# A queue-order planner without a reserve for the matrix engine, choosing among 60 orders

## The chip, the cores and the metric

The kernel runs on one core of one Trainium2 chip. The metric is the time of one execution on the device in microseconds (us); lower is better. The core's engines work side by side, each through its own queue in order: PE (TensorE, matrix products and transposes), DVE (VectorE), ACT (ScalarE), POOL (GpSimd), and SP (SyncE), which only issues transfers (DMA). PE reads its operands from SBUF and writes to eight PSUM banks, named `bk0` to `bk7` here.

## The reference, cut to what matters

One step of a four-layer trunk, D = 2048, on 128 context tokens and 256 latent tokens. Layers 0 and 3 mix with windowed attention, layer 1 with neighbourhood attention (16 heads of 128 each), layer 2 with a gated MLP.

```python
for i in range(DEPTH):                      # 4 layers, mixer i % 3
    kind = i % N_MIXERS
    sh, sc, gt = split(silu(cond) @ w_ada[i] + b_ada[i], 3)   # for c_ctx and for c
    h = rmsnorm(x, norm_g[i]) * (1 + sc) + sh
    if kind in (0, 1):                      # window / neighbourhood attention
        q, k, v, z = split(h @ w_in)
        y = (attention(rmsnorm(q), rmsnorm(k), v, cache) * silu(z)) @ w_out
    else:                                   # gMLP in chunks of 128 positions
        u, v, z = split(h @ w_in)           # gelu on u and v
        y = (u * mix(layernorm(v)) * silu(z)) @ w_out
    x = x + gt * y
```

All data are 32-bit floats.

## The kernel before, in words

**Tiling.** x is held transposed, feature by token: 16 blocks of 128 x 384. Every weight comes as 128 x 1024 tiles of 512 KB into one of four buffers `raw`. Each tile is split in two by `split`: ACT writes the rounded `H`, DVE writes the remainder `L` = `raw` - `H` (three buffers of each). The activations are split likewise into `hH` and `hL`. A product is then three matmuls, hH·H, hL·H and hH·L, added up in a PSUM bank. These matmuls of a layer's weights are called the main stream below.

**Attention heads.** Beside the main stream of layers 0, 1 and 3 run the 16 heads of that layer. A head (`head`) comes to PE in pieces that are here called chunks: transposes of q into a bank; the scores (`bk<-pair,qT`), which need `qT` and `qc` from DVE and ACT; seven transposes of the normalized weights `Pt` or `PH` (heads alternate between these two tiles); then the product with v (`bk<-pc,cv`, `bk<-PTH,pair`, `bk<-PLT,pair`), which needs `PTH` and `pc` from ACT and `PLT` from DVE. Between scores and transposes DVE and ACT do the softmax: row maxima into `sm`, exponentials, the RECIPROCAL of the sums, and the scaling of `Pt`. At a layer's end stands `W_out`: its results leave the bank by DVE's `pair<-bk,ada,pair` (gate times product, added to x).

**The modulation stream ("ada rows").** The modulation vectors of layers 1 to 3 are mostly made without PE: 272 tiles `araw` of w_ada, for each a DVE product `prod<-araw,cbc` for one condition and `araw<-araw,cbc` for the other, each summed by an ACT instruction with an accumulator; the sums go through `accA` to `ada`. These 544 DVE and 544 ACT instructions are not urgent: each layer's vectors are read only when the layer before it ends.

**What sets the order.** The kernel is first written out by generators in program order, and class `Rec` only records each operation. `Rec.cost` gives a modelled duration, `add` the dependencies. `due` works out, back from PE's times, by when each operation must have begun for PE not to wait. `schedule` then simulates the five engines and picks, on each engine, from the operations whose inputs are there: PE takes them in program order (chunks of heads may move against the main stream), the others the one that is due first. `ready_at` says when an operation's inputs are there: the end of the producer plus `SEM` = 45 ns when it is on another engine, and for PE's operations `MARGIN` = 250 ns more. `order` runs `due` and `schedule` three times, each from the times of the last, and `emit` issues the operations in the order of the planned starts. All recorded instructions therefore bear one line of the code: 322 before, 355 after. The planner runs when the kernel is built; on the chip the queues run by themselves, and an operation that comes to the head of its queue too early waits there, with all behind it.

Of the kernel before, what the change touches and what calls it, by code (L numbers as in the profile page):

```python
# [3 lines left out]

# [45 lines left out]
class Rec:  # L50
# [162 lines left out]
                have = set(x for x, _ in self.dep[c])  # L213
                self.dep[c] += [(x, d) for x, d in self.dep[i] if x < c and x not in have]

    def ready_at(self, i, start, done, margin=0):
        t, e = 0.0, self.eng[i]
        for x, data in self.dep[i]:
            v = start[x] + 1
            if data:  # L220
                v = done[x] + (35 if self.eng[x] == e else self.SEM if e else self.SEM + margin)
            if v > t:
                t = v
        return t
# [28 lines left out]
                    late[x] = v  # L253
        return late

    MARGIN = 250

    def schedule(self, late, land=4000):
        n = len(self.ops)
        succ, left = [[] for _ in range(n)], [0] * n  # L260
        for i in range(n):
            left[i] = len(self.dep[i])
            for x, _ in self.dep[i]:
                succ[x].append(i)
        start, done = [0.0] * n, [0.0] * n
        free, dma = [0.0] * 5, 0.0
        wait, ready = [[] for _ in range(5)], [[] for _ in range(5)]
        key = [(float(i) if self.chunk[i] == i else -1.0) if self.eng[i] == 0 else late[i] for i in range(n)]
        for i in range(n):
            if not left[i]:  # L270
                heapq.heappush(wait[self.eng[i]], (0.0, i))
        count = 0
        while count < n:
            best, be = None, None
            for e in range(5):
                if ready[e]:
                    t = free[e]
                elif wait[e]:
                    t = max(free[e], wait[e][0][0])
                else:  # L280
                    continue
                if best is None or t < best:
                    best, be = t, e
            e, t = be, best
            while wait[e] and wait[e][0][0] <= t:
                i = heapq.heappop(wait[e])[1]
                heapq.heappush(ready[e], (key[i], i))
            i = ready[e][0][1]
            if e in (1, 2) and wait[e]:
                end, hold = t + self.dur[i], None  # L290
                for est, j in wait[e]:
                    if est < end and late[j] < end and late[j] < late[i] and (hold is None or est < hold):
                        hold = est
                if hold is not None:
                    free[e] = hold
                    continue
            heapq.heappop(ready[e])
            start[i] = t
            free[e] = t + self.dur[i]
            if self.load[i]:  # L300
                dma = max(dma, t + 700) + self.load[i]
                done[i] = max(dma + land, t + self.lat[i])
            else:
                done[i] = t + self.lat[i]
            count += 1
            for s in succ[i]:
                left[s] -= 1
                if not left[s]:
                    heapq.heappush(wait[self.eng[s]], (self.ready_at(s, start, done, self.MARGIN), s))
        return start, done  # L310

    def order(self, passes=3):
        self.join()
        start, done = self.in_order()
        for _ in range(passes):
            start, done = self.schedule(self.due(start))
        return sorted(range(len(self.ops)), key=lambda i: (start[i], i))

    def emit(self):
        for i in self.order():  # L320
# [1443 lines left out]
```

## Time and profile before

| what | before |
|---|---|
| runs, median (lowest to highest) | 2989.2 us (2988.85 to 2990.47), 3 runs |
| profiled execution, its own time | 2990.54 us |
| its span in the trace | 2988.7 us |
| PE busy, share of the span | 2954.1 us, 99% |
| DVE busy | 2127.0 us, 71% |
| ACT busy | 1742.6 us, 58% |
| mean granted clock of PE | 0.997 |

A busy share is an average over the span: DVE is at nine tenths or more in most of the first half and at half of that afterwards. PE's waits are listed with what released them. The granted clock is given as a share of 2.4 GHz; 0.5 is the other level, 1.2 GHz, and a value between is a stretch that holds some of both. A row `L322 PE MATMUL bk<-hH,H ...` reads: line, engine, operation, tile written, tiles read.

### The profile page before, as it was taken

Reading aid. Unit: us, or ns where it says so; the run is one execution under the profiler, and the core shown is the slowest. Engines: PE = TensorE matmul, PEld = TensorE weight load, DVE = VectorE, ACT = ScalarE, POOL = GpSimd, SP = SyncE. Lnnn points to the kernel's source line nnn. Section 1 sums busy time; section 2 is a strip of 40 time slices with the busy share of each in tenths; the row PEclk is TensorE's granted clock in tenths of the full one; section 3 lists DMA queues with packets and bytes.
Section 4 is the critical chain, followed back from the end, with each engine's and each line's share of the span. In section 5 each row is a group of like instructions: output and inputs, shape, how many; then the busy total and the mean of one; then the engine's idle time right before and its main releaser. Section 6 shows DMA issues by size and latency. Waiting matters only on the chain.

```text
span 2988.7 us, 43977 instructions
## 1 busy us (share of the span) xinstructions
PE 2954.1 (99%) x16504; PEld 2703.4 (90%) x16504; DVE 2127.0 (71%) x3158; ACT 1742.6 (58%) x3340; POOL 79.9 (3%) x45
## 2 busy tenths in 40 slices
PE   7999999999999999999999999999999999999999
PEld 4789999978888888997888999999999988899999
DVE  4599999989989999998994833433455456455664
ACT  3388888778888888777883222222233235454542
POOL 0000000000101010000000000000000000000000
PEclk9999999999999999999999999999999999999999
DMA  9866677867776777887774544344454454333433
GB/s 379 343 227 220 201 236 251 279 242 257 235 252 234 257 239 255 286 263 287 260 260 134 176 128 124 124 126 128 124 169 141 144 191 134 123 106 106 138 111 126
DMA packets 187359, 598.96 MB, mean 200 GB/s; under 512 B 21764, under 2 KB 47620, under 8 KB 187140
## 3 DMA queue, kind: packets, MB, share of 16 engines
q1 hardware_dynamic: 186712, 596.00, 59.8%
q8 instruction: 129, 2.11, 0.3%
q14 instruction: 86, 0.70, 0.1%
q10 hardware_dynamic: 432, 0.13, 0.0%
HBM read 580.31 MB, written 15.75 MB: 199 GB/s over the span
## 4 chain that ended last, share of the span: by engine, by line
PE 95%; DVE 2%; ACT 1%; DMA 1%; issue 1%; DVEq 0%; SPq 0%; ACTq 0%
PE bk L322 95%; DVE prod L322 0%; DVE L L322 0%; DVE pair L322 0%; DVE Pt L322 0%; DMA pair<-i_xT 0%; ACT prod L322 0%; ACT Pt L322 0%; DMA aux<-i_relb 0%; DMA sel<-i_sel 0%; ACT H L322 0%; DVE PH L322 0%; DVE PLT L322 0%; ACT PH L322 0%; DVE araw L322 0%
## 5 line engine op out<-in xcount | busy, mean ns | idle before, releaser
L322 ACT ACTIVATE H<-raw 128x1024 fp32r<-128x1024 f32 x640 | 677.7, 1059 | 957.3 <-PE bk L322 887.7
L322 DVE TENSOR_TENSOR L<-raw,H 128x1024 fp32r<-128x1024 f32 x640 | 784.6, 1226 | 465.7 <-ACT H L322 460.7
L322 PE MATMUL bk<-hH,H 128*128 128x384 f32 x3072 | 1035.7, 337 | 5.5 <-DVE pair L322 5.4
L322 PE MATMUL bk<-hH,L 128*128 128x384 f32 x3072 | 1028.5, 335 | 0.0
L322 PE MATMUL bk<-hL,H 128*128 128x384 f32 x3072 | 1027.8, 335 | 0.0
L322 PE MATMUL bk<-H,hH 128*128 128x512 f32 x1536 | 605.6, 394 | 6.8 <-ACT hH L322 5.4
L322 PE MATMUL bk<-H,hL 128*128 128x512 f32 x1536 | 601.1, 391 | 0.3 <-DVE hL L322 0.3
L322 PE MATMUL bk<-L,hH 128*128 128x512 f32 x1536 | 600.6, 391 | 0.1
L322 PEld LDWEIGHTS bk<-hH,H 128*128 128x128 f32 x3072 | 577.1, 188 | 15.1 <-DVE pair L322 7.4
L322 PEld LDWEIGHTS bk<-hL,H 128*128 128x128 f32 x3072 | 577.2, 188 | 0.7
L322 PEld LDWEIGHTS bk<-hH,L 128*128 128x128 f32 x3072 | 576.9, 188 | 0.4 <-DVE cbc L322 0.4
L322 PEld LDWEIGHTS bk<-H,hH 128*128 128x128 f32 x1536 | 289.1, 188 | 71.5 <-ACT hH L322 6.6
L322 DVE TENSOR_TENSOR prod<-araw,cbc 128x1024 f32<-128x1024 f32 x272 | 335.6, 1234 | 16.6 <-ACT prod L322 11.4
L322 PEld LDWEIGHTS bk<-H,hL 128*128 128x128 f32 x1536 | 288.9, 188 | 64.2 <-issue 1.3
L322 PEld LDWEIGHTS bk<-L,hH 128*128 128x128 f32 x1536 | 289.2, 188 | 57.9 <-issue 1.3
L322 DVE TENSOR_TENSOR araw<-araw,cbc 128x1024 f32<-128x1024 f32 x272 | 335.4, 1234 | 5.0 <-DMA cbc<-srow 1.5
L322 ACT ACTIVATE prod<-prod 128x1024 f32<-128x1024 f32 x272 | 287.1, 1055 | 62.6 <-DVE prod L322 52.3
L322 ACT ACTIVATE araw<-araw 128x1024 f32<-128x1024 f32 x272 | 286.8, 1054 | 39.2 <-DVE araw L322 38.3
L322 DVE SCALAR_TENSOR_TENSOR pair<-bk,ada,pair 128x256 f32<-128x256 f32 x320 | 119.1, 412 | 178.1 <-PE bk L322 177.9
L322 ACT ACTIVATE pair<-bk 128x512 f32<-128x512 f32 (+2 forms) x150 | 82.0, 556 | 22.4 <-PE bk L322 21.9
L322 DVE TENSOR_TENSOR PLT<-bk,aux 128x384 f32<-128x384 f32 x32 | 17.8, 557 | 73.4 <-PE bk L322 73.3
L322 DVE TENSOR_TENSOR pair<-pair,aux 128x512 f32<-128x512 f32 (+1 forms) x108 | 59.1, 589 | 12.2 <-ACT pair L322 11.9
(152 smaller groups left out, 2048.6 us busy)
## 6 DMA issues: line engine op xcount, KB each, us to landing
araw<-i_w_adaT SPq DMA_DIRECT2D x272, 512.0 KB, 4.4
raw<-i_win_B SPq DMA_DIRECT2D x96, 512.0 KB, 3.7
raw<-i_nat_B SPq DMA_DIRECT2D x96, 512.0 KB, 4.3
pair<-i_w_ada SPq DMA_DIRECT2D x77, 512.0 KB, 7.2
raw<-i_win_O SPq DMA_DIRECT2D x64, 512.0 KB, 3.8
raw<-i_gm_V SPq DMA_DIRECT2D x64, 512.0 KB, 4.3
raw<-i_gm_U SPq DMA_DIRECT2D x64, 512.0 KB, 3.6
raw<-i_gm_Z SPq DMA_DIRECT2D x64, 512.0 KB, 3.6
```

The costliest lines, as they stand in the source:

```text
L322: getattr(getattr(self.real, e), op)(*a, **k)
```

## The change

`MARGIN` is gone: PE's operations count as ready 45 ns after their last producer, as those of the other engines do. `order` makes 60 orders instead of 3. Six come from the old iteration, each from the times of the last. For the other 54, the due times of the best order so far are shifted at random by up to 1.2 us either way, for the operations of DVE, ACT, POOL and SP that start in the 200 us before a random point, and a new order is planned from them. Every order gets a mark: the planned end, plus the ends of three trials (`trial`), which replay the order with durations up to 3% longer, results up to 120 ns later and loads landing after 3000 instead of 4000 ns. The order with the lowest mark is issued. The recorded operations and their dependencies are the same as before; only their places in the queues differ.

```diff
-    def ready_at(self, i, start, done, margin=0):
+    def ready_at(self, i, start, done):
...
-                v = done[x] + (35 if self.eng[x] == e else self.SEM if e else self.SEM + margin)
+                v = done[x] + (35 if self.eng[x] == e else self.SEM)
...
-    MARGIN = 250
+    def trial(self, order, seed):
+
+        rnd = random.Random(seed)
+        free, dma = [0.0] * 5, 0.0
+        start, done = [0.0] * len(order), [0.0] * len(order)
+        for i in order:
+            e = self.eng[i]
+            t = max(free[e], self.ready_at(i, start, done))
+            start[i] = t
+            more = self.dur[i] * 0.03 * rnd.random() if e else 0
+            free[e] = t + self.dur[i] + more
+            if self.load[i]:
+                dma = max(dma, t + 700) + self.load[i]
+                done[i] = max(dma + 3000, t + self.lat[i])
+            else:
+                done[i] = t + self.lat[i] + more + (120 * rnd.random() if e else 0)
+        return max(done)
...
-                    heapq.heappush(wait[self.eng[s]], (self.ready_at(s, start, done, self.MARGIN), s))
+                    heapq.heappush(wait[self.eng[s]], (self.ready_at(s, start, done), s))
...
-    def order(self, passes=3):
+    def order(self, passes=60):
         self.join()
+        rnd = random.Random(1)
         start, done = self.in_order()
-        for _ in range(passes):
-            start, done = self.schedule(self.due(start))
-        return sorted(range(len(self.ops)), key=lambda i: (start[i], i))
+        best = None
+        for n in range(passes):
+            if n < 6:
+                late = self.due(start)
+            else:
+                w = max(done) * rnd.random()
+                late = [x + (rnd.random() - 0.5) * 2400 if self.eng[i] and 0 < w - start[i] < 2e5 else x
+                        for i, x in enumerate(best[2])]
+            new, done = self.schedule(late)
+            o = sorted(range(len(self.ops)), key=lambda i: (new[i], i))
+            end = max(done) + sum(self.trial(o, k) for k in range(3))
+            if n < 6:
+                start = new
+            if best is None or end < best[0]:
+                best, start = (end, o, late), new
+        return best[1]
```

**Place 1, PE at the end of layer 0's heads.** From the scores of one head (tile `qT`) to the transposes of `Pt_228`, the normalized weights of the head before it, and on to that head's product with v. Before:

```order
L322 MATMUL bk4_118<-pair3_169_296,qT_79 128x384
L322 MATMUL bk5_119<-ident_84,Pt_228_355 128x128 x4
L322 MATMUL bk2_116<-ident_84,Pt_228_355 128x128 x3
L322 MATMUL bk6_120<-hH_65,H0_71 128x384
L322 MATMUL bk6_120<-hL_66,H0_71 128x384
L322 MATMUL bk6_120<-hH_65,L0_74 128x384
L322 MATMUL bk6_120<-hH_65,H0_71 128x384
L322 MATMUL bk6_120<-hL_66,H0_71 128x384
L322 MATMUL bk6_120<-hH_65,L0_74 128x384
L322 MATMUL bk5_119<-pc_81,cv_160_287 128x128
```

And now:

```order
L355 MATMUL bk4_118<-pair3_169_296,qT_79 128x384
L355 MATMUL bk1_115<-hL_66,H2_73 128x384
L355 MATMUL bk1_115<-hH_65,L2_76 128x384
L355 MATMUL bk1_115<-hH_65,H2_73 128x384
L355 MATMUL bk1_115<-hL_66,H2_73 128x384
L355 MATMUL bk1_115<-hH_65,L2_76 128x384
L355 MATMUL bk1_115<-hH_65,H2_73 128x384
L355 MATMUL bk5_119<-ident_84,Pt_228_355 128x128 x4
L355 MATMUL bk2_116<-ident_84,Pt_228_355 128x128 x3
L355 MATMUL bk1_115<-hL_66,H2_73 128x384
L355 MATMUL bk1_115<-hH_65,L2_76 128x384
```

Before, nothing stood between the scores and the transposes, and 6 matmuls of the main stream between the transposes and `bk5<-pc,cv`; now 6 stand ahead of the transposes and 18 behind them, and the transposes are PE's row 2062 where they were row 2082.

**Place 2, DVE in layer 1.** From the RECIPROCAL of a head's sums to that head's `PLT_377`, with `L0`, `L1` for the main stream and ada rows (`prod`, `araw`) in between. Before:

```order
L322 RECIPROCAL sm0_106<-sm0_106 128x3
L322 TENSOR_SCALAR Pt_375_502<-Pt_375_502,sm0_106 128x384
L322 TENSOR_TENSOR prod_77<-araw2_322_449,cbc_78 128x1024
L322 TENSOR_TENSOR araw2_322_449<-araw2_322_449,cbc_78 128x1024
L322 TENSOR_TENSOR L0_74<-raw3_70,H0_71 128x1024
L322 TENSOR_TENSOR prod_77<-araw0_323_450,cbc_78 128x1024
L322 TENSOR_TENSOR araw0_323_450<-araw0_323_450,cbc_78 128x1024
L322 TENSOR_TENSOR L1_75<-raw0_67,H1_72 128x1024
L322 TENSOR_TENSOR PLT_377_504<-bk5_119,PTH_376_503 128x512
L322 TENSOR_TENSOR PLT_377_504<-bk6_120,PTH_376_503 128x256
```

And now:

```order
L355 RECIPROCAL sm0_106<-sm0_106 128x3
L355 TENSOR_SCALAR Pt_375_502<-Pt_375_502,sm0_106 128x384
L355 TENSOR_TENSOR L0_74<-raw3_70,H0_71 128x1024
L355 TENSOR_TENSOR prod_77<-araw0_317_444,cbc_78 128x1024
L355 TENSOR_TENSOR L1_75<-raw0_67,H1_72 128x1024
L355 TENSOR_TENSOR PLT_377_504<-bk5_119,PTH_376_503 128x512
L355 TENSOR_TENSOR PLT_377_504<-bk6_120,PTH_376_503 128x256
```

Of four ada rows between the two, one is left; the others stand later in DVE's queue.

**Place 3, PE where layer 1's last heads meet W_out.** Around the transposes of `Pt_415` and the use of bank `bk0` by W_out (`hH`, `hL` against `H1`, `L1`). Before:

```order
L322 MATMUL bk7_121<-ident_84,Pt_415_542 128x128 x4
L322 MATMUL bk4_118<-ident_84,Pt_415_542 128x128 x3
L322 MATMUL bk0_114<-hH_65,H1_72 128x384
L322 MATMUL bk0_114<-hL_66,H1_72 128x384
L322 MATMUL bk0_114<-hH_65,L1_75 128x384
L322 MATMUL bk0_114<-hH_65,H1_72 128x384
L322 MATMUL bk0_114<-hL_66,H1_72 128x384
L322 MATMUL bk0_114<-hH_65,L1_75 128x384
L322 MATMUL bk6_120<-pc_81,cv_346_473 128x128
```

And now, from the last rows of the transposes on:

```order
L355 MATMUL bk4_118<-ident_84,Pt_415_542 128x128 x3
L355 MATMUL bk3_117<-hL_66,H0_71 128x384
L355 MATMUL bk3_117<-hH_65,L0_74 128x384
L355 MATMUL bk3_117<-hH_65,H0_71 128x384
...
L355 MATMUL bk6_120<-pc_81,cv_346_473 128x128
...
L355 MATMUL bk4_118<-pair4_402_529,qT_79 128x384
L355 MATMUL bk0_114<-hH_65,H1_72 128x384
L355 MATMUL bk0_114<-hL_66,H1_72 128x384
L355 MATMUL bk0_114<-hH_65,L1_75 128x384
```

The first matmul into `bk0` stood right behind the transposes; now 11 matmuls into `bk3`, the head's product with v and the next head's scores stand ahead of it.

Over the whole program the ada rows on DVE drift back: at the end of layer 0's heads 3 fewer of them are done than before, by the end of layer 1's about 17, and the last stands some 20 rows later in a queue of 2,900.

## Rows read from the trace of the kernel before

**Rows 1.** The page's first part: busy time, share of the span, instructions.

```profile
PE 2954.1 (99%) x16504; PEld 2703.4 (90%) x16504; DVE 2127.0 (71%) x3158; ACT 1742.6 (58%) x3340; POOL 79.9 (3%) x45
```

**Rows 2.** PE's waits over the span: releaser, us in total, times, longest us.

```profile
PE bk L322 <- DVE spad L322: 11.3, 1, 11.3
PE bk L322 <- DVE pair L322: 5.9, 6, 1.9
PE bk L322 <- ACT hH L322: 5.4, 4, 2.0
PE bk L322 <- ACT Pt L322: 2.2, 1, 2.2
PE bk L322 <- DMA pair<-i_w_ada: 2.1, 1, 2.1
PE bk L322 <- DVE PLT L322: 1.4, 2, 1.2
PE bk L322 <- ACT pair L322: 0.9, 1, 0.9
```

**Rows 3.** Stretches: length; busy of PE, PEld, DVE, ACT, POOL; clock; DMA share, GB/s.

```profile
75.00:1572.00 1497.00, 1481.99 (x8014) 1307.51 (x8007) 1371.07 (x1939) 1196.97 (x2423) 63.74 (x31) 0.99 0.74 254
1572.00:2988.70 1416.70, 1412.42 (x8078) 1360.05 (x8076) 719.36 (x1149) 515.90 (x869) 14.55 (x7) 1.00 0.43 134
```

**Rows 4.** The page's costliest groups: busy, mean ns of one, idle before.

```profile
L322 DVE TENSOR_TENSOR L<-raw,H 128x1024 fp32r<-128x1024 f32 x640 | 784.6, 1226 | 465.7 <-ACT H L322 460.7
...
L322 DVE TENSOR_TENSOR prod<-araw,cbc 128x1024 f32<-128x1024 f32 x272 | 335.6, 1234 | 16.6 <-ACT prod L322 11.4
```

**Rows 5.** Timeline at place 1: start us, us, engine, what; idle before and releaser.

```profile
475.77 1.23 DVE L322 TENSOR_TENSOR L<-raw,H 128x1024 fp32r<-128x1024 f32 x1
...
478.08 0.64 ACT L322 ACTIVATE Pt<-Pt,sm 128x384 f32<-128x384 f32 x1
...
478.57 1.21 DVE L322 TENSOR_TENSOR prod<-araw,cbc 128x1024 f32<-128x1024 f32 x1
...
478.78 0.98 PE L322 MATMUL bk<-ident,Pt 128*128 128x128 f32 x7 [2.18 <-ACT Pt L322]
...
480.49 0.57 PE L322 MATMUL bk<-hH,H 128*128 128x384 f32 x1 [0.73 <-DVE pair L322]
```

**Rows 6.** Stretches right behind waits, columns as in rows 3.

```profile
480.50:484.00 3.50, 3.50 (x14) 3.50 (x15) 3.50 (x11) 1.47 (x5) 0.00 (x0) 0.52 1.01 394
...
612.00:621.00 9.00, 7.00 (x29) 3.42 (x29) 7.14 (x20) 5.38 (x13) 0.00 (x0) 0.62 0.68 269
...
1227.30:1231.00 3.70, 3.70 (x18) 3.70 (x19) 3.26 (x7) 1.92 (x4) 0.00 (x0) 0.62 0.73 235
...
895.00:952.00 57.00, 54.94 (x285) 47.73 (x284) 54.77 (x75) 46.24 (x99) 4.97 (x3) 1.00 0.67 225
```

**Rows 7.** Timeline at place 2, columns as in rows 5.

```profile
935.25 1.29 POOL L322 TENSOR_TENSOR aux<-aux,mask 128x512 f32<-128x512 f32 x1 [17.76 <-DVE L L322]
935.35 2.27 DVE L322 TENSOR_TENSOR prod<-araw,cbc 128x1024 f32<-128x1024 f32 x1 [0.17 <-ACT prod L322]
...
939.93 1.02 DVE L322 TENSOR_TENSOR PLT<-bk,PTH 128x512 fp32r<-128x512 f32 x2
...
940.68 0.38 PE L322 MATMUL bk<-PLT,pair 128*128 128x256 f32 x1 [1.17 <-DVE PLT L322]
```

**Rows 8.** Timeline of DVE and of PE at place 3, columns as in rows 5.

```profile
1225.31 1.23 DVE L322 TENSOR_TENSOR prod<-araw,cbc 128x1024 f32<-128x1024 f32 x1
...
1227.24 0.45 PE L322 MATMUL bk<-hH,H 128*128 128x384 f32 x1 [1.95 <-DVE pair L322]
```

**Rows 9.** PE's waits from 148 to 173 us, columns as in rows 2.

```profile
PE bk L322 <- DVE pair L322: 3.2, 4, 1.2
```

**Rows 10.** Timeline of a chunk in mid-layer 0: its producer and PE.

```profile
456.13 1.02 DVE L322 TENSOR_TENSOR PLT<-bk,PTH 128x512 fp32r<-128x512 f32 x2
...
457.61 0.38 PE L322 MATMUL bk<-pc,cv 128*128 128x128 f32 x2
```

More of the change, by code (lines that the diff above doesn't have):

```diff
@@ L1 @@
 import heapq
+import random
 import re
```

## The prediction

> **What bounds the kernel now.** I read the page first, then PE's waits, then the stretches around them, then the instructions. The page shows PE busy for 2954.1 of 2988.7 us [rows 1], so 34.6 us of the span are idle and no order of the queues can give back more than that, plus what a slower clock costs. The list of PE's waits says where the idle time lies [rows 2]: 11.3 us on the first vector work of the program and 2.1 us on the first weights are the start-up, which has nothing queued ahead that could be ordered otherwise; the other five rows add up to 15.8 us (5.9 + 5.4 + 2.2 + 1.4 + 0.9), each wait 2.2 us or less. The stretches tell why the waits lie where they do [rows 3]: from 75 to 1572 us DVE is busy for 1371.1 of 1497 us, 92%, and PE idles for 15.0 us; afterwards DVE is busy for half of the time and PE idles for 4.3 us. What fills DVE in the first half beside the `L` tiles is the ada stream, 544 instructions of about 1.23 us [rows 4], and that stream is not urgent. So the question is whether the new orders keep ada rows, and `L` tiles that are due later, from standing ahead of what PE waits for.
>
> A wait costs more than its length. Behind the wait of 2.18 us at 478.78 us [rows 5] the granted clock is 0.52 for 3.5 us, that is the 1.2 GHz level, with PE busy throughout [rows 6]: work worth 3.5 x 0.52 = 1.8 us, so 1.7 us are lost. Behind the wait of 1.95 us at 1227.24 us [rows 8] it is 0.62 for 3.7 us, 1.4 us lost. In the stretch with a wait of 1.17 us [rows 7] the clock is 1.00 [rows 6], so the shorter waits cost their length alone.
>
> **The change part by part.** No operation is added or removed, so no duration changes; all of the effect is places in queues. I take each stretch in which PE waits.
>
> *Place 1, end of layer 0's heads.* PE waits 2.18 us for `Pt`, scaled by ACT until 478.72, then 0.73 us for a `pair` result behind an ada `prod` on DVE [rows 5]; with the clock's 1.7 us that is 4.6 us. The `Pt` chain stood behind an `L` of 1.23 us on DVE. In the new order six matmuls stand between the scores and the transposes where none stood, and eighteen instead of six behind them. One matmul of the main stream takes 0.175 us (8078 in 1412.4 us [rows 3]), so the six bring 1.05 us and the transposes' place in the program is 20 rows, 3.5 us, earlier against the main stream, whose later matmuls remain as cover. The bounds are 0 (the softmax is late by as much more) and -4.6; I take -4.0, near the upper gain, since more cover stands both ahead of and behind the chunk.
>
> *Place 2, layer 1.* PE waits 1.17 us for `PLT` [rows 7], and 0.9 us for a `pair` that ACT evacuates [rows 2]. On DVE four ada rows stood between the RECIPROCAL and this `PLT`; one is left. Three fewer are 3 x 1.23 = 3.7 us, more than the wait, though each also comes back elsewhere in a queue that is 92% full. Bounds 0 and -2.1; I take -1.8.
>
> *Place 3, layer 1's heads meet W_out.* PE waits 1.95 us for the release of `bk0`, which DVE does behind an ada `prod` that begins at 1225.31 and takes 1.23 us [rows 8]; with the clock 3.4 us. Now 11 matmuls, the head's product with v and the next scores stand ahead of `bk0`'s first matmul, so its release can be 2 to 3 us later. But the 11 matmuls (1.9 us) are all that covers ACT's `PTH` and DVE's `PLT`, the latter alone two instructions of 1.02 us together [rows 7]. A piece of 1.2 us ahead of them would bring back a wait of about 1 us. Bounds 0 and -3.4; I take -2.5.
>
> *Evacuations at 148 to 173 us.* Four waits, 3.2 us in all, the longest 1.2 us [rows 9]. One bank is drained by DVE between blocks and no more of PE's work is there to be put ahead. Bounds 0 and -3.2; I take -0.5, since the rows that differ here move no whole piece.
>
> *Transitions between layers.* Most of the 5.4 us on `hH` [rows 2], with a clock of 0.62 around 612 us [rows 6], lies where a layer's first activations are made one after the other. The order there is the same before and after: 0.
>
> *What the lost reserve costs.* In mid-layer a chunk starts at 457.61, 0.46 us after its `PLT` ended (456.13 + 1.02) [rows 10]; without the 0.25 us about 0.2 us should be left. The planner counts a whole chunk as ready when its last input is, and the chunk's first matmul does not read `PLT`; so the true spare is larger. New waits need lateness that the planner does not know. One kind is visible: at 935.35 an ada `prod` took 2.27 us instead of 1.23, having started 0.1 us behind a POOL instruction on `aux` [rows 4, 7]. A quarter of a microsecond would not have absorbed that. Bounds: 0, and 16 us if each of layer 1's 16 bias masks on POOL cost PE a full 1.0 us; I take +1.0, one such hit, because of the many in before one stands ahead of a wait of PE.
>
> The sum: -4.0 - 1.8 - 2.5 - 0.5 + 1.0 = -7.8 us. The profiled execution took 2990.54 us, 1.3 us above the median of the runs, an offset that the terms do not depend on; so 2989.2 - 7.8 = **2981.4 us**.
>
> **The rivals.**
>
> *The saved waits come back (half the gain).* DVE stays 92% full until the ada stream is done, and deferring it moves where its rows collide. The mechanism with a trace is the one at place 2: a DVE instruction with two operands in SBUF stretched from 1.23 to 2.27 us beside POOL's `aux` [rows 4, 7]. The new order puts other DVE instructions beside the 16 masks; four hits of 1.0 us on what PE waits for leave 2989.2 - 8.8 + 4 = 2984.4 us, and with one clock fall of 1.5 us 2986 us. For it: the planner's costs have no such term. Against: DVE's urgent pieces are the smaller part of its queue. The Trainium skill (SBUF — State Buffer, section "SBUF: two separate sides") says that DVE instructions with two SBUF inputs and GpSimd instructions that read SBUF share a port pair as an exclusive lock, whichever starts first holding it for its whole instruction. The trace agrees: POOL ends at 936.54, and 1.1 us later DVE is done. By that page every meeting costs up to a whole POOL instruction, 1.3 us here, and the gain is what the order happens to meet.
>
> *No effect.* The marks are made by the planner's own model; that an order is best there need not hold on the chip. Then the time stays at about 2989. Against: at all three places the rows moved in the direction that PE's waits ask for.
>
> *Slower.* The reserve was what kept small lateness from PE. There are 48 heads with 4 chunks each, 192 chunks. If one in seven, 27, now has one piece of 1.2 us too many ahead of it, with 0.2 us spare, 27 x 1.0 = 27 us are lost and the time is 2989.2 - 8.8 + 27 = 3007 us. It decides from 15 such chunks on (8.8 + 6 us). For it: DVE's 92%. Against: PE's present waits are 0.7 to 2.2 us, with the reserve; they are whole pieces out of place, which 0.25 us neither caused nor prevented, and the chunks that start on time show no use of it.
>
> *Everything goes.* If the start-up evacuations and the smaller waits went too, 15.8 us and 3.1 us of clock would be the floor: 2989.2 - 18.9 = 2970 us. All three places whole with no new wait, 10.1 us, give 2979; half-way to the floor is 2974.5.
>
> **How the numbers follow.** Forecast, 2977 to 2985: chance 0.52; waits come back, 2984 to 2987: 0.20; no effect: 0.06; everything goes, below 2977: 0.14; slower: 0.08. A measurement of this kernel can tell some 0.2%, 6 us, from no change, so faster means below 2983.2. Of the forecast 0.40 lies there, of the first rival 0.06, and all of the fourth: 0.60. Slower by over 6 us is the slower rival and a little of the forecast's tail: 0.09. The rest, 0.31, is within. The range leaves out half of the 0.14 below and the slower rival above: from 2974.5 to 2990.5, the upper end being no change plus the 1.3 us by which runs here differ.
>
> **What would show it.** Right: PE's wait for `Pt` near 478 us and the one on `bk0` near 1227 us are below 1 us and the clock is 1.00 in the 4 us behind them; PE's waits sum to about 23 us instead of 30; the waits on `hH` at the layers' ends stay at about 2 us; DVE's ada rows end some 15 to 25 us later. Place 2 is wrong if `PLT` still waits with one ada row ahead. The forecast is wrong if PE's list of waits shows new entries of over 0.5 us in layers 0, 1 or 3, above all behind DVE instructions of over 2 us, or if PE's idle time falls and its clock falls with it.

## The result and the profile after

| what | before | after |
|---|---|---|
| runs, median (lowest to highest) | 2989.0 us (2986.7 to 2990.5), 4 runs | 2970.5 us (2969.7 to 2974.8), 4 runs |
| profiled execution, its own time | 2990.54 us | 2969.68 us |
| its span | 2988.7 us | 2967.9 us |

The ratio of the runs is 0.9942, 95% interval 0.9924 to 0.9959: 18.5 us faster by the medians, 20.8 us between the two traces. The forecast was 2981.4 us in a range from 2974.5 to 2990.5; the time lies 4 us below the range. It is close to what the prediction gave as the floor, 2970 us, but by chance: some of the waits counted in the floor are still there, and other terms were larger.

The page of the kernel after, first part (as in rows 1), and the chain that ended last:

```profile
PE 2942.6 (99%) x16504; PEld 2698.0 (91%) x16504; DVE 2126.3 (72%) x3158; ACT 1741.4 (59%) x3340; POOL 79.4 (3%) x45
...
PE 99%; DMA 0%; DVE 0%; ACT 0%; issue 0%; SPq 0%; DVEq 0%; ACTq 0%
```

The span fell by 20.8 us, PE's idle time by only 9.3 us (34.6 to 25.3). The other 11.5 us is busy time of PE: the same 16504 matmuls took 2954.1 us before [rows 1] and 2942.6 us now. So half of the gain is not in the list of waits at all. Much of it is the clock: the stretches of 3.5, 9.0 and 3.7 us in rows 6 lose 1.7, 3.4 and 1.4 us by their clocks of 0.52, 0.62 and 0.62, and 5.2 us at 0.67 at the start of layer 2 (below) another 1.7. That makes some 8 us, an estimate, and the kernel after has none of it: its clock is 1.00 in both halves. The list, answering rows 2:

```profile
PE bk L355 <- DVE spad L355: 11.0, 1, 11.0
PE bk L355 <- ACT hH L355: 4.3, 4, 1.4
PE bk L355 <- DVE pair L355: 2.7, 3, 1.4
PE bk L355 <- DMA pair<-i_w_ada: 2.1, 1, 2.1
PE bk L355 <- ACT PTH L355: 1.0, 2, 0.5
PE bk L355 <- DVE PLT L355: 0.2, 1, 0.2
```

The waits for `Pt` and for ACT's `pair` are gone, `pair` fell from 5.9 to 2.7 us, `hH` from 5.4 to 4.3 us with a longest of 1.4 instead of 2.0. Nothing new is over 0.5 us. The stretches of rows 3, and then those of the three places (columns: length; busy of PE, PEld, DVE, ACT, POOL; clock; DMA share, GB/s):

```profile
75.00:1572.00 1497.00, 1491.76 (x8091) 1319.10 (x8088) 1369.57 (x1937) 1194.07 (x2414) 63.24 (x31) 1.00 0.75 255
1572.00:2967.90 1395.90, 1391.68 (x7989) 1343.28 (x7987) 720.29 (x1151) 517.70 (x878) 14.55 (x7) 1.00 0.44 135
466.00:490.00 24.00, 24.00 (x157) 23.92 (x156) 23.57 (x48) 18.92 (x45) 0.00 (x0) 1.00 0.72 254
920.00:940.00 20.00, 20.00 (x103) 17.06 (x102) 16.77 (x27) 16.24 (x41) 1.41 (x1) 1.00 0.63 220
...
1205.00:1220.00 15.00, 15.00 (x96) 14.92 (x95) 13.62 (x34) 11.68 (x29) 0.00 (x0) 1.00 0.80 255
```

At all three places PE is busy without a gap and at the 2.4 GHz level. DVE is as full as before, 1369.6 of 1497 us: the gain came without emptying DVE.

**Where the 20.8 us came from.** The same main-stream matmul starts at a certain time in either trace; the difference, read at points between the places (the median over the matmuls within 2.5 us), steps at six points. In us gained (the last column is the second trace of the changed kernel, from the experiments):

| stretch of the trace before | foretold | after | the same kernel, another execution |
|---|---|---|---|
| place 1 (430 to 500) | 4.0 | 5.9 | 5.9 |
| start of layer 1 (605 to 630) | 0 | 2.9 | 2.9 |
| place 2 (935 to 960) | 1.8 | 2.6 | 2.6 |
| place 3 (1200 to 1250) | 2.5 | 4.0 | 4.0 |
| start of layer 2 (1250 to 1380) | 0 | 3.5 | 1.4 |
| start of layer 3 (2445 to 2475) | 0 | 0.7 | 0.7 |
| all else, evacuations and new waits among it | -0.5 | 1.2 | 0.8 |
| sum | 7.8 | 20.8 | 18.3 |

### The profile page after: what moved, and what is told of

Read it like the earlier page. It is cut to its first block, busy times and chain, and to the rows that moved or that the text cites. A ratio compares the mean times of both kernels' runs of the same rounds, so it can differ in the third digit from the quotient of the medians.

```text
span 2967.9 us, 43952 instructions
## 1 busy us (share of the span) xinstructions
PE 2942.6 (99%) x16504; PEld 2698.0 (91%) x16504; DVE 2126.3 (72%) x3158; ACT 1741.4 (59%) x3340; POOL 79.4 (3%) x45
## 4 chain that ended last, share of the span: by engine, by line
PE 99%; DMA 0%; DVE 0%; ACT 0%; issue 0%; SPq 0%; DVEq 0%; ACTq 0%
PE bk L355 99%; DMA pair<-i_xT 0%; DMA sel<-i_sel 0%; DVE Pt L355 0%; ACT Pt L355 0%; DVE pair L355 0%; ACT hH L355 0%; DVE PLT L355 0%; ACT PLT L355 0%; DVE L L355 0%; ACT H L355 0%; ACT PTH L355 0%; ACT PH L355 0%; DVE PH L355 0%; SPq L355 0%
## 5 line engine op out<-in xcount | busy, mean ns | idle before, releaser
L355 PEld LDWEIGHTS bk<-hH,H 128*128 128x128 f32 x3072 | 577.0, 188 | 11.9 <-DVE pair L355 4.7
L355 DVE SCALAR_TENSOR_TENSOR pair<-bk,ada,pair 128x256 f32<-128x256 f32 (+1 forms) x320 | 119.2, 412 | 174.9 <-PE bk L355 174.8
L355 DVE TENSOR_TENSOR pair<-pair,aux 128x512 f32<-128x512 f32 (+1 forms) x108 | 59.3, 587 | 11.6 <-ACT pair L355 11.5
```

The costliest lines, as they stand in the source:

```text
L355: getattr(getattr(self.real, e), op)(*a, **k)
```

## The starts of layers 1 and 2

This is the largest miss. Before, at the start of layer 1 (start us, us, engine, what, idle and releaser):

```profile
606.33 0.81 PE L322 MATMUL bk<-ones,PTH 128*128 128x1 f32 x6
...
607.39 1.22 DVE L322 TENSOR_TENSOR araw<-araw,cbc 128x1024 f32<-128x1024 f32 x1
...
608.53 0.15 DVE L322 TENSOR_SCALAR st<-bk 128x3 f32<-128x3 f32 x1
...
611.06 0.59 PE L322 MATMUL bk<-pair,sT 128*2 128x256 f32 x2
...
614.20 0.80 PE L322 MATMUL bk<-H,hH 128*128 128x512 f32 x1 [2.00 <-ACT hH L322]
```

And after:

```profile
599.70 0.81 PE L355 MATMUL bk<-ones,PTH 128*128 128x1 f32 x6
...
600.54 0.16 DVE L355 TENSOR_SCALAR st<-bk 128x3 f32<-128x3 f32 x1 [0.36 <-PE bk L355]
...
604.28 1.46 PE L355 MATMUL bk<-pair,sT 128*2 128x256 f32 x18
...
607.41 0.50 PE L355 MATMUL bk<-H,hH 128*128 128x512 f32 x1 [1.14 <-ACT hH L355]
```

The chain is: sum of squares on PE (`ones,PTH`), `st` on DVE, a power on POOL, the broadcast on PE (`PH,ones`), then ACT, DVE and ACT until `hH`. PE fills its time with matmuls on `sT`, the modulation that is made on PE. Before, `st` stood behind an ada row on DVE and began 2.2 us after `ones,PTH`; now it begins 0.84 us after, as soon as PE is done. In PE's order 19 matmuls on `sT`, counted from those on `spad`, stood ahead of the broadcast and 1 behind the start of it; now 9 ahead and 11 behind (each is two rows of the trace). It is as many matmuls, but those behind the broadcast cover the last link of the chain. The wait fell from 2.00 to 1.14 us, and the clock did not fall behind it: 0.62 from 612 to 621 us before [rows 6], and now (start of layer 1, start of layer 2):

```profile
606.00:612.00 6.00, 4.86 (x32) 2.62 (x32) 5.99 (x17) 4.97 (x12) 0.00 (x0) 1.00 0.84 328
1343.00:1349.00 6.00, 4.74 (x31) 2.49 (x31) 6.00 (x18) 5.28 (x13) 0.00 (x0) 1.00 0.87 319
```

One would take the 0.9 us by which the wait is shorter for time saved. It is not: from `ones,PTH` to the first `hH` matmul PE takes 7.87 us before (606.33 to 614.20) and 7.71 us now (599.70 to 607.41). The chain is nearly as long as it was; the work was only moved into its last pause, so that PE's idle time is in smaller pieces. What was saved lies behind the first `hH`. The next 25 rows of PE are the same work in both kernels, 9 matmuls of the main stream and 8 matmuls on `sT`. Before, then after, at the start of layer 1 and of layer 2 (columns: length; busy of PE; clock; DMA share, GB/s):

```profile
614.20:620.67 6.47, 6.47 (x25) 0.51 0.61 234
1363.12:1368.31 5.19, 5.19 (x26) 0.67 0.50 196
```

```profile
607.41:611.22 3.81, 3.81 (x26) 1.00 0.91 351
1344.40:1348.20 3.80, 3.80 (x26) 1.00 0.91 322
```

So of the 2.9 us at the start of layer 1 the clock behind the wait is 2.7 us, and the shorter way to the first `hH` 0.2. At the start of layer 2 it is 1.4 of 3.5 us; there the first `hH` itself comes 2.1 us earlier against the main stream.

## The experiments

Twelve kernels ran, each in 5 to 11 executions beside the kernel before. Gains by place are read as in the table above, between the profiled execution of each kernel and that of the kernel before. One execution carries an error of some 1 to 3 us in the sum, mostly from the program's start: up to 100 us the traces already differ by up to 3 us. And the kernel before has a single trace, of an execution of 2990.5 us; its medians beside these runs are 2988.2 to 2988.4 us. So some 2 us of each row's sum may belong to that one execution, and no run shows at which place.

| kernel | median, us | ratio to before, interval | place 1 | start of layer 1 | place 2 | place 3 | start of layer 2 |
|---|---|---|---|---|---|---|---|
| changed kernel again | 2972.6 | 0.9950 (0.9937 to 0.9962) | 5.9 | 2.9 | 2.6 | 4.0 | 1.4 |
| other start of the random numbers | 2974.7 | 0.9954 (0.9941 to 0.9966) | 5.9 | 2.1 | 2.6 | 3.9 | 0.7 |
| 400 orders | 2974.1 | 0.9953 (0.9941 to 0.9966) | 5.8 | 2.8 | 2.6 | 3.9 | 3.3 |
| mark without trials | 2975.1 | 0.9957 (0.9943 to 0.9970) | 4.6 | 3.2 | 2.2 | 3.8 | 3.1 |
| no reserve, best of 6 orders | 2974.4 | 0.9954 (0.9942 to 0.9967) | 5.0 | 3.6 | 2.5 | 2.6 | 3.8 |
| no reserve, three iterations | 2976.6 | 0.9964 (0.9952 to 0.9977) | 5.1 | 3.2 | 2.5 | 3.1 | -0.6 |
| reserve 100 ns, three iterations | 2981.3 | 0.9979 (0.9970 to 0.9987) | 1.0 | -0.2 | 1.7 | 2.7 | 2.9 |
| reserve 500 ns, three iterations | 2988.3 | 1.0003 (0.9994 to 1.0012) | 3.3 | 0.3 | 2.6 | -1.7 | 0.4 |
| reserve 250 ns, 60 orders, trials | 2985.6 | 0.9991 (0.9982 to 0.9999) | -0.2 | -0.1 | 2.5 | 0.3 | 2.1 |
| reserve dropped at layer starts alone | 2985.2 | 0.9993 (0.9984 to 1.0002) | 1.8 | 2.8 | 1.8 | -0.2 | 2.1 |
| reserve kept at layer starts alone | 2982.8 | 0.9981 (0.9972 to 0.9990) | 4.6 | 0.1 | 2.2 | 2.5 | 0.7 |
| changed kernel, ACT delayed at layer starts | 2980.3 | 0.9972 (0.9962 to 0.9982) | 5.9 | -0.2 | 2.6 | 4.0 | -0.5 |

### Reserve or search?

Two theories: R, the absence of the reserve brings most of the gain; S, the choice among marked orders does.

The search with the reserve put back:

```diff
+    MARGIN = 250
...
-    def ready_at(self, i, start, done):
+    def ready_at(self, i, start, done, margin=0):
...
-                v = done[x] + (35 if self.eng[x] == e else self.SEM)
+                v = done[x] + (35 if self.eng[x] == e else self.SEM if e else self.SEM + margin)
...
-                    heapq.heappush(wait[self.eng[s]], (self.ready_at(s, start, done), s))
+                    heapq.heappush(wait[self.eng[s]], (self.ready_at(s, start, done, self.MARGIN), s))
```

> The changed kernel's search (60 orders, three trials) with the reserve of 250 ns put back. Theory R (the reserve made PE's planned order too cautious, and its absence brings most of the 18.5 us): little is left, 0 to 5 us faster than before, and PE's waits on hH near the layers' first matmuls stay at about 2.0 us with the clock at 0.5 to 0.6 behind them. Theory S (choosing among 60 marked orders brings most): 12 to 18 us faster than before, with those waits as short as in the changed kernel (1.1 to 1.4 us).

2985.6 us, ratio 0.9991: 2.9 us faster than before, as R said. The wait at the start of layer 1 is untouched, and so is the clock behind it:

```profile
614.82 0.79 PE L357 MATMUL bk<-H,hH 128*128 128x512 f32 x1 [2.00 <-ACT hH L357]
```

```profile
614.80:618.80 4.00, 3.98 (x14) 1.78 (x14) 4.00 (x10) 2.36 (x5) 0.00 (x0) 0.50 0.94 364
```

The kernel before without the reserve, and nothing else:

```diff
-    MARGIN = 250
+    MARGIN = 0
```

> The kernel before with the reserve set to 0 and nothing else: three iterations, the last order taken. Theory R: 10 to 16 us faster than before; the waits at 478 us, 1227 us and at the layers' first matmuls shrink below 1.5 us. Theory S: 0 to 5 us faster. The slower rival of the prediction (late inputs at many chunks): 5 us slower or more, with new entries in PE's list of waits.

2976.6 us: 11.9 us faster, some two thirds of the 18.5, in the range that R gave. The wait at 478 us is gone and that at the start of layer 1 is 0.83 us. At the start of layer 2 it was not as R expected: the wait on `hH` there is 2.0 us, as before, and the clock behind it at 0.50:

```profile
PE bk L322 <- ACT hH L322: 4.7, 4, 2.0
```

```profile
1348.50:1352.50 4.00, 3.96 (x17) 1.56 (x21) 3.75 (x10) 1.85 (x4) 0.00 (x0) 0.50 0.94 372
```

Six orders without reserve, the best by the mark:

```diff
-    def order(self, passes=60):
+    def order(self, passes=6):
```

> The changed kernel with only its first 6 orders, of which the best mark is taken, so without the 54 random shifts. Theory R: within 4 us of the changed kernel (14 to 18 us faster than before). Theory S: at most 5 us faster than before, as the random shifts are left out.

2974.4 us, 14.0 us faster than before and 1.8 to 3.9 us behind the changed kernel's two medians (2972.6 and 2970.5). Against the three iterations the start of layer 2 is what it gained in the trace (3.8 instead of -0.6 us), and PE's order differs there: 3 matmuls on `sT` stand behind the broadcast with three iterations, 11 with six. Three iterations, then six orders:

```profile
1345.40 0.61 PE L322 MATMUL bk<-pair,sT 128*2 128x256 f32 x6
```

```profile
1344.69 1.47 PE L355 MATMUL bk<-pair,sT 128*2 128x256 f32 x22
```

So taking the best order instead of the last one kept an order that is better there. That the whole program is faster by it is not shown, as the intervals overlap.

The mark without the trials:

```diff
-            end = max(done) + sum(self.trial(o, k) for k in range(3))
+            end = max(done)
```

> The changed kernel with the mark made of the planned end alone, the three trials left out. If the trials choose an order that stands up to lateness on the chip: 4 us or more slower than the changed kernel, with waits of 0.5 to 1 us at chunks that the changed kernel does not show. If they do not matter: within 2 us of the changed kernel.

2975.1 us, 2.5 us behind the changed kernel's later runs, between the two expectations. Its list of waits shows one of 1.0 us at 478 us that the changed kernel has not, which speaks for the trials; the intervals overlap (0.9943 to 0.9970 against 0.9937 to 0.9962), so their worth is not shown.

Other shifts, and more of them:

```diff
-        rnd = random.Random(1)
+        rnd = random.Random(2)
```

> The changed kernel with another start of the random numbers, so other shifts and another chosen order. If what the reserve's absence brings is there in any such order: within 3 us of the changed kernel. If the changed kernel's time is the luck of one order: 5 us or more slower than it.

```diff
-    def order(self, passes=60):
+    def order(self, passes=400):
```

> The changed kernel with 400 orders instead of 60. If the search has more to give on the chip: 3 us or more faster than the changed kernel. If it is used up (what remains of PE's waits is the start and the chain of the layers' first activations): within 2 us.

2974.7 and 2974.1 us. Neither is told apart from the changed kernel by its interval. The search is used up; no version here beats the changed kernel.

> The changed kernel itself, beside the three that follow, so that they are compared on one chip. 2968 to 2976 us; ratio to before 0.993 to 0.996. It settles whether the 2 to 6 us by which it led the kernels without search or trials are real: if the search is worth something, it is 3 us or more faster here than those were (2974.4 to 2976.6 us); if not, it is within 2 us of them.

2972.6 us, ratio 0.9950. The kernels with 6 to 400 orders and no reserve lie between 0.9950 and 0.9957, all inside one another's intervals. Against the kernels without search or trials it is 1.8 to 4.0 us faster, which falls between the two expectations. What the runs support: the reserve's absence is worth 11.9 us of the 18.5. All the rest, the best instead of the last order among it, makes 4 to 6 us by the medians, but its interval overlaps that of the three iterations (0.9937 to 0.9962 against 0.9952 to 0.9977), so no part of it is shown alone.

### The same order, two executions

The changed kernel's second profile gained 2.1 us less at the start of layer 2 than its first. First execution, then second, DVE and PE:

```profile
1340.89 1.23 DVE L355 TENSOR_TENSOR prod<-araw,cbc 128x1024 f32<-128x1024 f32 x1 [0.49 <-DMA araw<-i_w_adaT]
...
1344.40 0.50 PE L355 MATMUL bk<-H,hH 128*128 128x512 f32 x1 [1.26 <-ACT hH L355]
```

```profile
1342.44 1.22 DVE L355 TENSOR_TENSOR prod<-araw,cbc 128x1024 f32<-128x1024 f32 x1 [1.59 <-DMA araw<-i_w_adaT]
...
1343.59 1.01 DVE L355 TENSOR_TENSOR Pt<-pair,bk 128x384 f32<-128x384 f32 x2
...
1345.79 0.79 PE L355 MATMUL bk<-H,hH 128*128 128x512 f32 x1 [2.20 <-ACT hH L355]
```

```profile
1345.80:1349.80 4.00, 4.00 (x16) 2.07 (x16) 4.00 (x10) 2.99 (x6) 0.00 (x0) 0.64 0.69 270
```

An ada row stands ahead of `Pt` in DVE's queue. Its tile came 1.1 us later in the second execution (idle 1.59 instead of 0.49 us), and the chain behind it came 0.9 us later: PE's wait went from 1.26 to 2.20 us and the clock to 0.64. A row that is not urgent cost 2.1 us in the one execution against the other, because its load was late and it stood at the head of DVE's queue.

### The reserve's size

```diff
-    MARGIN = 250
+    MARGIN = 500
```

> The kernel before with the reserve doubled to 500 ns, three iterations. Theory R: the loss grows with the reserve, 4 to 15 us slower than before. Theory S: within 3 us of before. If the reserve protects PE from lateness: faster than before.

2988.3 us, ratio 1.0003: no change. R expected 4 to 15 us slower and is wrong in that; nor does a larger reserve gain anything. The waits only changed places (3.3 us gained at place 1, 1.7 us lost at place 3).

```diff
-    MARGIN = 250
+    MARGIN = 100
```

> The kernel before with a reserve of 100 ns, three iterations. If the loss grows with the reserve: between before and the run without reserve, 4 to 8 us faster than before. If any reserve spoils the places (a threshold): within 3 us of before.

2981.3 us, 6.9 us faster, between 0 and 250 ns. So the loss grows up to 250 ns (5.0 us at 100 and 11.9 us at 250 ns against none, each measured beside the kernel before) and no more after that. Why it stops there is open.

### Where the reserve acts

The reserve dropped for PE's instructions at the layer starts alone, then the counterpart:

```diff
+        self.edge.append(any(s and s[0] in ("ones", "sel", "sT", "spad") for s in r))
...
-                    heapq.heappush(wait[self.eng[s]], (self.ready_at(s, start, done, self.MARGIN), s))
+                    heapq.heappush(wait[self.eng[s]], (self.ready_at(s, start, done, 0 if self.edge[s] else self.MARGIN), s))
```

> The kernel before with the reserve dropped for the PE instructions around a layer's start alone (those that read ones, sel, sT or spad), kept for all others; three iterations. If the gain of 7 us at the three layer starts comes from the reserve on these instructions: 4 to 8 us faster than before, the waits on hH there 1.0 to 1.5 us and the clock 1.00 behind them, while the waits at 478 us and 1227 us stay as in rows 5 and 8. If it comes from elsewhere (the queue of DVE and ACT running ahead, or the search): within 2 us of before and the waits at 2.0 us.

```diff
+        self.edge.append(any(s and s[0] in ("ones", "sel", "sT", "spad") for s in r))
...
-                    heapq.heappush(wait[self.eng[s]], (self.ready_at(s, start, done, self.MARGIN), s))
+                    heapq.heappush(wait[self.eng[s]], (self.ready_at(s, start, done, self.MARGIN if self.edge[s] else 0), s))
```

> The counterpart of the run with the reserve dropped at the layers' starts alone: the kernel before with the reserve kept at 250 ns there and dropped for all other PE instructions, three iterations. If the reserve acts in each place on its own: the places at 478, 940 and 1227 us gain 8 to 10 us as in the run without reserve, the starts of layers 1 and 2 nothing (waits of 2.0 us, clock at 0.5 to 0.7); 7 to 10 us faster than before. If the places depend on one another: another split.

Dropped there alone: 3.1 us faster (ratio 0.9993, its interval just holds 1), below the 4 to 8 expected. The trace shows the place: the wait at the start of layer 1 is 1.46 us and the clock behind it 1.00, a gain of 2.8 us, while the wait on `Pt` near 478 us is 2.32 us. Kept there alone: 5.4 us faster, below 7 to 10; the start of layer 1 is back at 2.21 us and the clock at 0.69, and place 1 gains 4.6 us. Rows of the one, then of the other:

```profile
614.93 0.50 PE L323 MATMUL bk<-H,hH 128*128 128x512 f32 x1 [1.46 <-ACT hH L323]
```

```profile
614.90:618.90 4.00, 3.97 (x21) 2.50 (x22) 4.00 (x11) 3.03 (x7) 0.00 (x0) 1.00 0.65 252
```

```profile
609.16 0.50 PE L323 MATMUL bk<-H,hH 128*128 128x512 f32 x1 [2.21 <-ACT hH L323]
```

```profile
609.10:613.10 4.00, 3.94 (x16) 1.72 (x16) 4.00 (x11) 2.40 (x6) 0.00 (x0) 0.69 0.96 370
```

Each part of the reserve does its harm at its own place: so it is at layer 1's start (2.8 us without it, 0.1 with it), at place 1 (4.6 and 1.8) and at place 3 (2.5 and -0.2). The start of layer 2 does not follow the reserve: it gains 2.1 and 2.9 us in two kernels with a reserve there (250 ns with the search, and 100 ns) and loses 0.6 us in one without any. The two sums, 3.1 and 5.4, make 8.5 of 11.9 us. The intervals are wide enough for the two to add up, but the traces also show smaller losses elsewhere (2 us and more between 630 and 900 us) that are not explained.

Place 2 gains 1.7 to 2.6 us in every kernel of the table, with any reserve, so it is not due to the reserve or the search: every other order was better there. What stood against PE in the order before were two ada rows and an `L` without a pause ahead of `PLT`, the first of them stretched beside POOL [rows 7]:

```profile
937.66 1.23 DVE L322 TENSOR_TENSOR araw<-araw,cbc 128x1024 f32<-128x1024 f32 x1
938.80 1.22 DVE L322 TENSOR_TENSOR L<-raw,H 128x1024 fp32r<-128x1024 f32 x1
```

The stretch is 1.04 us (2.27 instead of 1.23), the wait behind these rows 1.17 us. In eight of the other traces a DVE instruction is stretched there too, to 2.2 us or more, and PE does not wait for `PLT` at that place.

### What a longer wait costs

Five copies on ACT ahead of the first `hH` of layers 1, 2 and 3, in the changed kernel:

```diff
+            if i in self.slow:
+                for _ in range(5):
+                    self.real.scalar.activation(self.late[0], self.late[1], AF.Copy)
             getattr(getattr(self.real, e), op)(*a, **k)
...
+            if p == 0 and l:
+                self.nc.slow.add(len(self.nc.ops))
+                self.nc.late = self.junk, self.ident
             self.act(h, self.htmp[p % 3])
```

> The changed kernel with five extra copies on ACT (about 1.0 us together, results not used) right ahead of the first hH of layers 1, 2 and 3. PE then waits about 1.0 us longer at each. If a wait's price is its length: 3 us slower than the changed kernel. If waits of about 2 us bring the clock down and shorter ones do not: the first two (1.1 and 1.3 us before) go to 2.1 and 2.3 us and lose 1.5 to 2 us more each by a clock at about 0.5, the third (0.5 us) goes to 1.5 us and loses nothing more: 6 to 7 us slower.

The copies took 1.66 us, not 1.0. The waits at the three starts, and the 4 us behind each:

```profile
611.99 0.50 PE L359 MATMUL bk<-H,hH 128*128 128x512 f32 x1 [2.70 <-ACT hH L359]
...
1351.60 0.80 PE L359 MATMUL bk<-H,hH 128*128 128x512 f32 x1 [2.62 <-ACT hH L359]
...
2450.66 0.79 PE L359 MATMUL bk<-H,hH 128*128 128x512 f32 x1 [2.05 <-ACT hH L359]
```

```profile
612.00:616.00 4.00, 4.00 (x23) 1.64 (x23) 4.00 (x10) 2.34 (x5) 0.00 (x0) 0.71 0.55 207
1351.60:1355.60 4.00, 4.00 (x15) 2.11 (x16) 4.00 (x10) 2.99 (x6) 0.00 (x0) 0.50 0.53 197
2450.60:2454.60 4.00, 3.94 (x14) 2.10 (x15) 3.08 (x8) 2.10 (x6) 0.00 (x0) 0.50 0.35 110
```

The waits grew by 1.56, 1.36 and 1.55 us against the changed kernel's first trace, 4.5 us in all; the three places lost 3.1, 4.0 and 4.4 us, 11.5 us. So a wait's price is not its length: in this execution 4.5 us of waiting took 11.5 us, the rest being the clock. But it is the slowest of eight, 2983.9 us at a mean clock of 0.997. The median is 2980.3 us, 7.7 us above that of the changed kernel's later runs and 9.8 us above its first, and two executions at 0.999 took 2976.0 us, 3.4 and 5.5 us above these two medians, about the length of the waits alone. The number expected, 6 to 7 us, was too low because the delay was longer and because the third wait reached the fall too.

## Why the prediction was wrong, point by point

- **What bounds the kernel** held: PE's waits and the clock behind them, in the first half, are where the time came from. An ada row stood in the way of `st` at the start of layer 1 as well, but `st` came 1.4 us sooner and the first `hH` only 0.2.
- **The step that failed** is "Transitions between layers ... The order there is the same before and after: 0". I compared the chain on ACT and DVE from the broadcast to `hH`, which is the same, and not PE's own order around it, nor `st` ahead of it. The order of PE had changed there, and the trace of before had already shown the price: a wait of 2.0 us and a clock of 0.62 over 9 us [rows 2, 6]. Reckoned as at places 1 and 3, that clock alone is 9.0 x 0.38 = 3.4 us; 2.7 us of it came back. The starts are worth 7.1 us in the two traces (2.9, 3.5 and 0.7), 7.1 of the 13.0 by which the sum missed. Of the 3.5 at the start of layer 2 some is luck: the same kernel's second trace has 1.4.
- **The sizes at places 1 to 3** were too small by 1.9, 0.8 and 1.5 us, and all three lie above the bounds that I gave as the most (4.6, 2.1 and 3.4). The mechanism was right, the bound was not. A wait in the list runs from the drawn end of the matmul before, and a matmul is drawn 0.335 us long where one follows another every 0.175 us; so each wait hides 0.16 us of lost time; "the shorter waits cost their length alone" was wrong by that much. PE's weight loads show it, at the two waits of rows 5:

```profile
478.77 0.75 PEld L322 LDWEIGHTS bk<-ident,Pt 128*128 128x128 f32 x7 [2.50 <-ACT Pt L322]
...
480.49 0.19 PEld L322 LDWEIGHTS bk<-hH,H 128*128 128x128 f32 x1 [0.96 <-DVE pair L322]
```

  2.50 and 0.96 us where the list has 2.18 and 0.73. With these place 1's bound is 5.1 us, and with the 0.3 us wait for `qc` ahead of them, which I left out, 5.4. The remaining 0.5 us of the 5.9 is not accounted for.
- **Evacuations**: 0.5 foretold, 0.6 read between 100 and 200 us. Right.
- **New waits from the lost reserve**: +1.0 foretold, none seen; the new entries in the list are 0.5 us or less. The rival "slower" rested on late chunks; with the reserve at 0 and three iterations there are none worth 1 us. The argument against it was half right. The waits were whole pieces out of place; but that 0.25 us "neither caused nor prevented" them is refuted, since with the reserve at 0 and nothing else changed the waits of 2.2 and 1.95 us near 478 and 1227 us are gone.
- **"The saved waits come back"** did not happen. The meetings of DVE and POOL go on, seven DVE instructions of over 1.8 us in layer 1 where there were ten, but PE waits behind none of them. For instance (DVE and POOL, then the stretch):

```profile
943.10 1.29 POOL L355 TENSOR_TENSOR aux<-aux,mask 128x512 f32<-128x512 f32 x1 [18.08 <-DMA aux<-i_relb]
943.26 2.20 DVE L355 TENSOR_TENSOR prod<-araw,cbc 128x1024 f32<-128x1024 f32 x1
```

```profile
940.00:950.00 10.00, 10.00 (x55) 8.54 (x54) 7.20 (x11) 8.92 (x25) 1.29 (x1) 1.00 0.68 216
```

  The rule of the Trainium skill (SBUF — State Buffer, "SBUF: two separate sides") that the two engines lock each other out holds in this trace too, 2.20 instead of 1.23 us beside a POOL instruction of 1.29 us; it had no part in the time after the change. Before, a stretched row stood in the chain that ended in the wait at place 2, as shown above.
- **What the reserve is.** I costed it as protection that is lost. It was an error of the model: the chip starts PE 0.06 us after the producer's end (478.72 to 478.78 [rows 5]), which the planner's 45 ns already holds, and the 250 ns on top let it send other matmuls ahead of a chunk that was in fact ready. Those were missing later as cover: 0 and 6 main-stream matmuls around `Pt_228` before, 6 and 18 now; 1 matmul on `sT` behind the broadcast before, 11 now. That the reserve brings about these waits, the runs show; that it does so by moving the cover is argued from the orders and the traces. At the start of layer 1 the moved cover did not shorten the chain, it kept the clock up.
- **The foretold signs**: the waits sum to 21.3 us (about 23 foretold), those near 478 and 1227 us are gone, the ada rows end 13.8 us later (15 to 25 foretold); the waits on `hH` did not stay at 2 us.

## What to carry to other kernels

A reserve in a planner is not free safety: on the engine that is the bound it hands out the cover too early, so set it to what the trace shows between a producer's end and the consumer's start. Taking the best of a few orders rather than the last may help too; here that is not told apart from noise. When an order changes, compare the bounding engine's own queue at every wait of the trace, also where the other engines' queues look the same. Cost a wait by the gap between the starts of its neighbours, plus what the clock loses behind it, and do not take a shorter wait in a list for time saved before the starts around it say so.

## What the runs showed of the hardware

- In six stretches of each of the fourteen traces (places 1 to 3 and the three layer starts), all 18 waits of PE from 1.93 to 2.70 us were followed by a mean granted clock of 0.73 or less over the next 4 us, 0.50 in six of them. Of those from 0.6 to 1.3 us with no longer one just ahead, one was (1.13 us, clock 0.67, at the start of layer 1 with other shifts); behind the others it was 1.00. Between 1.4 and 1.8 us it went both ways. Outside these stretches a wait of 0.81 us, 2.1 us behind one of 1.20, was followed by the lower level in one trace (reserve 100 ns, at 170 us); the kernel before has the same two waits there and kept 1.00.
- Executions of one program differ in how much of this they meet. Of 60 executions of the kernel before, 22 had a mean clock of 0.997 and took 2988.2 to 2993.9 us; 8 had 0.999 and took 2983.8 to 2986.7 us.
- That an execution of the same program can differ by 2.1 us at one place beside one load that lands 1.1 us later, the clock making over half of it, was not expected.
